# When the second gate pass starts, and how many of its steps stand in each v block

## The chip, the cores and the metric

The kernel runs on one core of a Trainium2 chip. The metric is the device time of one execution in microseconds. The core has a matrix engine (TensorE, PE in the profile), a vector engine (VectorE, DVE), a scalar engine (ScalarE, ACT), a general engine (GpSimd, POOL) and an engine that here issues transfers (SyncE, SP). Each has its own instruction stream, carried out in its written order; they wait for each other by semaphores. 16 DMA engines move data between HBM and on-chip memory.

## The reference

One decoder layer over 256 tokens of width 2048: attention in two head groups, a layer norm, a PEER block, a second norm, a gated per-layer embedding, and a third norm. All of it is in fp32. The change lies in the PEER block:

```
x   = LN1(alpha*x + concat(A, B) @ W_out)
q   = x @ peer_wq                      # 8 heads, two halves of 128
s1  = q[half 0] . keys[0] ; s2 = q[half 1] . keys[1]      # 128 keys each
top 16 of s1, top 16 of s2 -> 256 sums -> top 16          # per token and head
e   = ia*128 + ib                      # the expert's number, one of 16384
g   = softmax(the 16 sums)
h   = gelu(x . peer_u[e])              # one dot of 2048 per chosen expert
y   = sum over the 8*16 chosen of g*h*peer_v[e]
x   = LN2(alpha*x + y)
```

Every token thus needs 128 rows of `peer_u` and 128 rows of `peer_v`, 8 KB each.

## The kernel before, in words

**Two ways to do the experts.** Experts `e` are taken 128 at a time (a block, 1 MB of `peer_u` or `peer_v`). For most tokens the kernel computes whole blocks as matrix products: activations of all 128 experts of a block for all tokens (u part), multiplied by a gate matrix that is zero where a token did not choose the expert, then the product with the block's v rows (v part). A number of tokens (the natural or sparse ones) are done differently: their rows are gathered, one gather of 128 rows (1 MB, tile `gb`) at a time. 88 gathers of u rows each end in a dot on DVE (line 1012), 88 of v rows each in a step `y <- gb*ew + y` on DVE (line 1022). `gathers(n)`, called once a block with a table's number (`GU`, `GUL`, `GUE`, `GV`), spreads them over the blocks as background work; four `gb` tiles exist.

**Stages of the PEER block.** First the queries and their top 16, on DVE in `topk_work`, which also sends the sparse tokens' expert numbers to their slots (`head_slots`, transfers to `eig` issued by POOL). Then 56 direct u blocks (`u_block`), whose rows come in whole from SP's queue; their activations stand in the tiles A0 and A1. Then 48 listed u blocks: only experts that a token chose are in a list, and POOL's indirect DMA (`rows_of`, line 1409) fetches them by list into `uf` tiles; PE transposes them (1450) and multiplies them (1459), and the activations go to the tile `WL`. Then v: 39 blocks whose weights (`wc`) are gathered from the stored A0 and A1 (`s_w` in HBM), and 48 blocks whose weights are in `WL`; both by line 1505, sixteen matmuls a block, each against a 128-column piece of the block's rows (`vf` or `vx`). Five `vf` and `uf` tiles share slots; four `vx` tiles are used in the `wc` part.

**The gate passes.** `gate_work` makes the gate values for groups of three tokens. For each group DVE writes one-hots `eq` and `ohb` (line 717) and `lo` (1102), ACT writes `hi` (1100), PE multiplies them into a bank `ps_G` (1111, 1112), and DVE multiplies the activations by it (1120). The generator yields between these parts; a `run(work, n)` lets it go on by n steps. A full group takes two steps. Three or four groups are under way at a time. The first pass goes over A0 and A1 (56 groups) and, at the same time, finds each chosen expert's place in the list. Then A0 and A1 are stored to `s_w` (`stored = True`), the places are decoded, and the second pass (57 groups) goes over `WL`. In v, `half(d)` runs the second pass twice a block, after the eighth and the sixteenth matmul; the end of the pass must come before the first `WL` block.

**What sets the order.** DVE's and ACT's gate work and the y steps stand in the order in which the program text issues them (`keep`). PE's and POOL's instructions are placed by a planner at build time, and the placed order is fixed: an engine does not run ahead of an instruction that waits. In v two of the four banks used by `ps_G` hold sums of v, so that two are left for groups. POOL issues both the background gathers (line 1046) and all the blocks' fetches (1409) on one queue, one after another.

Of the kernel before, what the change touches and what calls it, by code (L numbers as in the profile page):

```python
# [19 lines left out]
P = 128  # L20
# [7 lines left out]
PH = 8  # L28
# [143 lines left out]
def build(tc, a, out):  # L172
# [7 lines left out]
    def pbank(pool, name, tag="bank", bufs=4):  # L180
        return pool.tile([P, 512], F32, name=name, tag=tag, bufs=bufs)
# [13 lines left out]
    at = pools.open("at", "left", bufs=2)  # L195
# [95 lines left out]
    def load(dst, src):  # L291
        tc.keep_in_program_order(nc.sync.dma_start(dst, src))
# [488 lines left out]
    def gates(t):  # L781

        g = gate[:, t]
        keep(nc.vector.tensor_tensor(g, CV[:, t], CV[:, t, :, 0:1].to_broadcast([P, PH, TOPK]),
                                     op=ALU.subtract))
        for _ in range(9):
            yield
        keep(nc.scalar.activation(g, g, AF.Exp))
        for _ in range(6):
            yield  # L790
        keep(nc.vector.tensor_reduce(gs[:, t], g, axis=AX.X, op=ALU.add))
        nc.vector.reciprocal(gs[:, t], gs[:, t])
        nc.vector.tensor_tensor(g, g, gs[:, t, :, None].to_broadcast([P, PH, TOPK]), op=ALU.mult)
        if t == 0:
            nc.vector.tensor_copy(eg[:NSPR, 1].bitcast(F32), g[:NSPR])
            for i in range(len(GROUPS)):
                slots(i, 1, by_slot(i, 1))
            gated.append(t)
        yield
# [3 lines left out]
    def slots(i, w, src):  # L803

        t0, n = GROUPS[i]
        nc.gpsimd.dma_start(eig[i][:, w],
                            src[t0:t0 + n].rearrange("t (r j) -> t r j", j=n))

    def by_slot(i, w):

        t0, n = GROUPS[i]

        buf, rows = (es, slice(t0, t0 + n)) if i < 2 else (es2, slice(GROUPS[1][0], NSPR))
        src = eg[rows, w].bitcast(F32)
        dst = buf[rows, w].bitcast(F32)
        nc.vector.tensor_copy(dst.rearrange("t (r h c) -> t h r c", h=PH, r=P // n),
                              src.rearrange("t h (r c) -> t h r c", r=P // n))
        return buf[:, w]

    def head_slots(h):  # L820

        c = slice(h * TOPK, (h + 1) * TOPK)
        nc.vector.scalar_tensor_tensor(eg[:NSPR, 0, h], iaN[:NSPR, 0, c], float(NKEY),
                                       ibN[:NSPR, 0, c], op0=ALU.mult, op1=ALU.add)
        t0, n = GROUPS[0]
        m = n // PH
        nc.gpsimd.dma_start(
            eig[0][:, 0, h * m:(h + 1) * m],
            eg[t0:t0 + n, 0, h].rearrange("t (r c) -> t r c", c=m))

    def topk_work():
        nc.vector.tensor_copy(io128, io128f)
        for h0, n in BATCH:
            for _ in topk_heads(0, h0, n):
                pass
            yield
            for h in range(h0, h0 + n):
                head_slots(h)
            yield
        for i in range(1, len(GROUPS)):  # L840
            slots(i, 0, by_slot(i, 0))

        second, first, flags = topk_heads(1, 0, PH), gates(0), first_flags()
        for step, _ in enumerate(second):
            if step > 2:
                next(first, None)
            if step > 5:
                next(flags, None)
            yield
        for _ in first:  # L850
            pass
        yield from index_T(1)
        yield from second_flags(gates(1), flags)

    def index_T(t):

        c = slice(t * P, (t + 1) * P)
        for src, dst, flat in ((iaN, iaT, iaF[:, c]), (ibN, ibT, None if t else ibF)):
            ps = pbank(pa, "ps_gT")
            keep(nc.tensor.transpose(ps[:, :P], src[:, t, :], ident))  # L860
            nc.scalar.copy(dst[:, c], ps[:, :P, None].to_broadcast([P, P, 2]))
            if flat is not None:
                nc.scalar.copy(flat, ps[:, :P])
            yield
# [28 lines left out]
    def first_flags():  # L893

        yield from index_T(0)
        cnt.append(pbank(pa, "ps_cnt")[:, :2 * P])
        keep(nc.tensor.matmul(cnt[0], ident, zero.to_broadcast([P, 2 * P]), start=True,
                              stop=False))
        for t0 in range(NSP, P, GB):
            n = min(GB, P - t0)  # L900
            oa, ob = (tkl.tile([P, GB, P], F16, name=nm, tag=nm) for nm in ("oa", "ob"))
            for j in range(n):
                act_one_hot(oa[:, j, :], tkl, iaF[:, t0 + j:t0 + j + 1])
                act_one_hot(ob[:, j, :], tkl, ibF[:, t0 + j:t0 + j + 1])
                if j or t0 % 5:
                    yield
            for j in range(n):
                count(t0 + j, ob[:, j, :], oa[:, j, :])
# [62 lines left out]
    def gathers(n):  # L971

        nonlocal due
        due += n
        while due >= 1:
            due -= 1
            run(sparse, 1)
# [222 lines left out]
    def all_gates(oh, A0, A1, WL):  # L1200

        places = Places(lkp, oh)
        yield from gate_work(oh, iaT, ibT, [(NSP, T, 0, SEG1, ((A0, NSP), (A1, NSP)))], places)
        a0 = 0
        for At in (A0, A1):
            for c in range(0, At.shape[1], 8):
                n = min(8, At.shape[1] - c)
                load(a["s_w"][1:, a0:a0 + n], At[:, c:c + n])
                a0 += n
                yield  # L1210
        nonlocal stored
        stored = True
        aT, bT = places.decode()
        yield
        nA, nB = CAPS[1]
        WA = WL[:, :nA * P].rearrange("p (b t) -> p b t", t=P)
        WB = WL[:, nA * P:].rearrange("p (b t) -> p b t", t=NDT)
        yield from gate_work(oh, aT, bT, [(NSP, P, nA, nB, ((WB, NSP),)),
                                          (P, T, 0, nA + nB, ((WA, P), (WB, NSP)))])
# [119 lines left out]
    def run(work, n):  # L1339

        for _ in range(n):
            if next(work, "end") == "end":
                return True
        return False


    def u_block(ia, dst):
        ps = pbank(pp, "ps_u")
        gemm_T32(su, a["peer_u"][ia], XF, ps, NSP, early[ia] if ia < EARLY else None)
        nc.scalar.activation(dst, ps[:, :NDT], AF.Gelu_apprx_tanh)  # L1350

    def W_of(ia):
        return A0[:, ia, :] if ia < SEG0 else A1[:, ia - SEG0, :]

    steps = 1
    work = topk_work()
# [26 lines left out]
    for ia in range(SEG1):  # L1383
        if ia == EARLY:
            pools.close("earlyp")
            a1p = pools.open("a1p", "right", bufs=1)
            A1 = a1p.tile([P, SEG1 - SEG0, NDT], F32, name="A1")
        u_block(ia, W_of(ia))
        run(work, steps + (steps == 1) * (ia % 2))
        gathers(0.9 if ia < EARLY else GU if steps == 1 else GUF if ia < SEG1 - 10 else GUT)  # L1390
    while not run(work, 1):
        pass
# [11 lines left out]
    def cols(i, b):  # L1404
        return (N0, P) if b < CAPS[i][0] else (0, NDT)
# [9 lines left out]
    def WL_of(b):  # L1415
        c0 = min(b, CAPS[1][0]) * P + max(b - CAPS[1][0], 0) * NDT
        return WL[:, c0:c0 + cols(1, b)[1]]
# [42 lines left out]
                             XF[:, d, NSP + c0:NSP + c0 + n], start=d == 0, stop=d == ND - 1)  # L1460

    stored = False
    work = all_gates(ohp, A0, A1, WL)
    rows = []
    turned = []

    def turn(k):
        b, c = divmod(k, 4)
        if b < NBLK[1]:
            if c == 0:  # L1470
                while len(rows) <= min(b + LEAD, NBLK[1] - 1):
                    rows.append(rows_of(slot("uf"), a["u_rows"], idxV[1], len(rows)))
            turned.append(rows_T(rows[b], c, pp, utp))
            if c == 3:
                rows[b] = None
# [3 lines left out]
    for b in range(NBLK[1]):  # L1479
        ps = pbank(pp, "ps_u")  # L1480
        c0, n = cols(1, b)
        for c in range(4):
            turn(4 * b + c + 2)
            rows_mm(ps, turned.pop(0), c, c0, n)
            if b >= 2 and (c or n > P) and not stored:
                run(work, 1)
        keep(nc.scalar.activation(WL_of(b), ps[:, :n], AF.Gelu_apprx_tanh))
        if b >= NBLK[1] - LEAD:
            fetch()
        gathers(GUL[n > P] if b < NBLK[1] - LEAD - 2 else GUE)  # L1490
# [46 lines left out]
    done = False  # L1537
    at = 0

    def half(d):  # L1540
        nonlocal done
        if not done:
            done = run(work, 1 + (d < 8 or at < 8))

    for b in range(NBLK[0]):
        if b == NBLK[0] - LEAD:
            more = nc.values_load(total[0:1, 0:1], min_val=0, max_val=NIA * NKEY)
        at = b
# [102 lines left out]
    with tc.If(more > 0, preferred_fallthrough_block=True, label="rest"):  # L1651
# [5 lines left out]
        for ia in range(NIA):  # L1657
            i = int(ia >= SEG1)
            vf, uf, _ = spare
# [397 lines left out]
```

## Time and profile before

| | |
|---|---|
| median of three runs | 1655.13 us (1651.96 to 1659.16) |
| profiled execution | 1654.64 us, span 1652.8 us |
| mean granted PE clock | 0.983 |
| PE, DVE, ACT, POOL busy | 97%, 64%, 44%, 35% of the span |
| DMA | 518.53 MB, mean 314 GB/s |
| direct u, listed u | about 560 to 816 us, 816 to 1132 us |
| v with `wc`, v with `WL` | 1136 to 1305 us, 1332 to about 1540 us |

Busy shares are averages over stages that have different limits. Times of stages are microseconds from the span's start, read from the timeline of PE. In a row of a timeline the first number is the start, the second the length; what stands in brackets at its end is the idle time before it and what ended it. `x` behind a row says how many instructions it groups. Waits are listed as total, count and longest.

### The profile page before, as it was taken

What the parts mean: (1) busy time and instruction counts of PE and PEld (TensorE: products, weight loads), DVE (VectorE), ACT (ScalarE), POOL (GpSimd) and SP (SyncE); (2) the same over time, 40 slices, a digit from 0 to 9 for tenths busy, and PEclk for the clock granted to TensorE, in tenths of its full rate; (3) what the DMA queues carried; (4) which work ended last, traced back from release to release, by engine and by line L of the source; (5) the groups of instructions that cost most, each with busy time, mean ns of one, the idle gap of its engine ahead of it and who ended that gap; (6) DMA issues with size and microseconds to landing.
All of it is one profiled execution on the core that took longest, in us unless ns stands there. A gap on an engine that the chain in (4) does not pass through costs nothing. (4 is left out here: it accounts for less than half of the span.)

```text
span 1652.8 us, 30585 instructions
## 1 busy us (share of the span) xinstructions
PE 1603.2 (97%) x11666; PEld 1486.8 (90%) x11666; DVE 1058.0 (64%) x2557; ACT 732.4 (44%) x1740; POOL 585.0 (35%) x542
## 2 busy tenths in 40 slices
PE   9999999999999999999989999999999679999998
PEld 7888888887888999999989999998999679999786
DVE  5555488855378899577678878842455762241776
ACT  5687458753101264857646666541032300000552
POOL 0133023201223423222464434447886455441000
PEclk9999999999999999999989999999999879999999
DMA  8554654485799799999999999999999899996661
GB/s 304 196 165 154 237 171 141 155 306 181 255 415 408 283 422 389 408 375 387 373 381 375 346 343 357 351 424 367 415 406 408 323 366 403 410 397 232 209 263 51
DMA packets 90614, 518.53 MB, mean 314 GB/s; under 512 B 12308, under 2 KB 15444, under 8 KB 38322
## 3 DMA queue, kind: packets, MB, share of 16 engines
q0 software_dynamic: 47984, 330.83, 50.9%
q1 hardware_dynamic: 40750, 182.55, 30.1%
q10 hardware_dynamic: 1728, 3.15, 0.5%
q8 instruction: 92, 1.51, 0.4%
q14 instruction: 60, 0.49, 0.1%
HBM read 508.47 MB, written 10.18 MB: 314 GB/s over the span
## 5 line engine op out<-in xcount | busy, mean ns | idle before, releaser
L133 DVE TENSOR_TENSOR wl<-wf,wh 128x1024 fp32r<-128x1024 f32 (+1 forms) x199 | 212.7, 1092 | 123.6 <-ACT wh L132 122.1
L132 ACT CAST wh<-wf 128x1024 fp32r<-128x1024 f32 (+1 forms) x199 | 172.1, 893 | 240.6 <-DMA wf<-ple_gate 128.7
L1022 DVE SCALAR_TENSOR_TENSOR y<-gb,ew,y 128x2048 f32<-128x2048 f32 x78 | 183.4, 2351 | 147.0 <-DMA gb<-v_rows,eig 146.6
L223 PE MATMUL ps_u<-XF,wf 128*128 128x168 f32 x1632 | 251.4, 310 | 1.5 <-DMA wf<-peer_u 1.4
L223 PEld LDWEIGHTS ps_u<-XF,wf 128*128 128x128 f32 x1632 | 234.5, 190 | 4.3 <-DMA wf<-peer_u 2.1
L1459 PE MATMUL ps_u<-XF,uT 128*128 128x128 f32 (+1 forms) x1536 | 222.5, 289 | 0.2 <-ACT uT L1453 0.2
L1012 DVE SCALAR_TENSOR_TENSOR gb<-gb,xq 128x2048 f32<-128x2048 f32 x88 | 200.7, 2285 | 21.3 <-DMA gb<-u_rows,eig 21.2
L1505 PE MATMUL ps_v<-WL,vf 128*128 128x128 f32 (+1 forms) x1536 | 197.1, 291 | 4.7 <-DVE WL L1120 4.5
L1459 PEld LDWEIGHTS ps_u<-XF,uT 128*128 128x128 f32 x1536 | 201.0, 193 | 0.5 <-ACT uT L1453 0.3
L1505 PEld LDWEIGHTS ps_v<-WL,vf 128*128 128x128 f32 x1536 | 195.3, 196 | 5.6 <-DVE WL L1120 4.7
L1046 POOL DMA_INDIRECT gb<-u_rows,eig x88 | 103.7, 1179 | 238.5 <-DVE gb L1012 56.5
L211 PE MATMUL ps_qk<-X,wh 128*128 128x512 f32 x512 | 185.2, 401 | 0.0
L1100 ACT ACTIVATE hi<-eq,ghf 128x56 f16<-128x56 f16 (+2 forms) x336 | 87.0, 325 | 166.0 <-DVE eq L717 162.1
L1453 ACT COPY uT<-ps_T 128x512 f32<-128x512 f32 x192 | 112.2, 587 | 109.2 <-PE ps_T L1450 109.0
L213 PE MATMUL ps_qk<-X,wl 128*128 128x256 f32 x512 | 145.7, 285 | 0.0
L1046 POOL DMA_INDIRECT gb<-v_rows,eig x88 | 121.5, 1381 | 66.2 <-DVE eq L717 24.0
L1409 POOL DMA_INDIRECT vf<-v_rows,idxV x73 | 90.3, 1237 | 114.3 <-PE ps_v L1505 84.0
L211 PEld LDWEIGHTS ps_qk<-X,wh 128*128 128x128 f32 x512 | 96.4, 188 | 22.0 <-issue 1.0
L1450 PE MATMUL ps_T<-ident,uf 128*128 128x128 f32 x768 | 115.1, 275 | 0.0
L223 PE MATMUL ps_q<-XF,wf 128*128 128x256 f32 x512 | 114.6, 382 | 0.0
L1505 PE MATMUL ps_v<-wc,vf 128*128 128x128 f32 (+1 forms) x800 | 106.4, 292 | 2.7 <-DMA vf<-v_rows,idxV 2.7
L223 PEld LDWEIGHTS ps_q<-XF,wf 128*128 128x128 f32 x512 | 96.4, 191 | 12.6 <-ACT eb L592 0.2
(366 smaller groups left out, 2855.2 us busy)
## 6 DMA issues: line engine op xcount, KB each, us to landing
wf<-peer_u SPq DMA_DIRECT2D x51, 1024.0 KB
wf<-w_qk SPq DMA_DIRECT2D x64, 512.0 KB
wf<-w_out SPq DMA_DIRECT2D x32, 512.0 KB
wf<-peer_wq SPq DMA_DIRECT2D x16, 1024.0 KB
wf<-ple_gate SPq DMA_DIRECT2D x16, 1024.0 KB
wf<-w_v SPq DMA_DIRECT2D x16, 512.0 KB
wf<-w_sv SPq DMA_DIRECT2D x15, 512.0 KB
early<-peer_u SPq DMA_DIRECT2D x5, 1024.0 KB
```

Of the source, the lines that this page charges most:

```text
L132: self.order(nc.scalar.copy(wh, src))
L133: self.order(nc.vector.tensor_tensor(wl, src, wh.bitcast(F32), op=ALU.subtract))
L211: nc.tensor.matmul(ps, wh[:, j * P:(j + 1) * P], xt[:, dt, :], start=dt == 0, stop=False)
L213: nc.tensor.matmul(ps[:, :T], wl[:, j * P:(j + 1) * P], xt[:, dt, :T], start=False, stop=dt == ND - 1)
L223: nc.tensor.matmul(ps[:, :T - t0], wf[:, dt * P:(dt + 1) * P], xt[:, dt, t0:], start=dt == 0, stop=dt == ND - 1)
L1012: keep(nc.vector.scalar_tensor_tensor(g, g, 1.0, xq[i], op0=ALU.mult, op1=ALU.mult, accum_out=eact[i][:, j:j + 1]))
L1022: keep(nc.vector.scalar_tensor_tensor(ys[i], g, ew[i][:, j:j + 1], ys[i], op0=ALU.mult, op1=ALU.add))
L1046: keep(nc.gpsimd.indirect_dma_start(out=g, out_offset=None, in_=a[kind], in_offset=bass.IndirectOffsetOnAxis(ap=eig[i][:, 0, j:j + 1], axi ...
L1450: nc.tensor.transpose(ps[:, j * P:(j + 1) * P], uf[:, (4 * c + j) * P:(4 * c + j + 1) * P], ident)
L1453: keep(nc.scalar.copy(uT, ps))
L1459: nc.tensor.matmul(ps[:, :n], uT[:, j * P:(j + 1) * P], XF[:, d, NSP + c0:NSP + c0 + n], start=d == 0, stop=d == ND - 1)
L1505: return nc.tensor.matmul(o, vf[:, d * P:(d + 1) * P], w, start=False, stop=last and (d % 3 == 2 or d == ND - 1))
```

## The change

Four edits, none of which changes what is computed.

1. In `topk_work` three more yields stand before the last batch's `head_slots`; three more steps are run in the first five direct u blocks.
2. The first gate pass starts at listed u block 4 where it started at block 2.
3. After the stores, one step of the second pass is run at the end of each listed u block, up to four (`begun`).
4. In v's first ten blocks `half` runs 3 + 2 steps a block, later 2 + 1; before, 2 + 2 in the first eight blocks, later 2 + 1.

```diff
@@ topk_work
             yield
+            if h0 + n == PH:
+                for _ in range(3):
+                    yield
             for h in range(h0, h0 + n):
                 head_slots(h)
             yield
@@ direct u blocks
-        run(work, steps + (steps == 1) * (ia % 2))
+        run(work, steps + (steps == 1) * (ia % 2 or ia < 5))
@@ listed u blocks
     stored = False
+    begun = 0
     work = all_gates(ohp, A0, A1, WL)
...
-            if b >= 2 and (c or n > P) and not stored:
+            if b >= 4 and (c or n > P) and not stored:
                 run(work, 1)
+        if stored and begun < 4:
+            begun += 1
+            run(work, 1)
@@ v, wc blocks
     def half(d):
         nonlocal done
         if not done:
-            done = run(work, 1 + (d < 8 or at < 8))
+            done = run(work, (3 if d < 8 else 2) if at < 10 else (2 if d < 8 else 1))
```

In the changed kernel all lines behind the first edit are higher by three to seven: 1409 is 1412, 1046 is 1049, 1111 is 1114, 1505 is 1512.

The instructions move most at three places. The first is POOL where listed u ends and v begins; `gb` is a background gather, `vf` and `vx` are rows of v blocks, `wc` their weights. Before:

```order
L1409 DMA vf<-v_rows,idxV_7967 128x2048
L1046 DMA gb<-v_rows,eig_4052 128x2048
L1409 DMA vf<-v_rows,idxV_7967 128x2048
L1046 DMA gb<-v_rows,eig_4052 128x2048
L1409 DMA vf<-v_rows,idxV_7967 128x2048
L1046 DMA gb<-v_rows,eig_4052 128x2048
L1409 DMA vf<-v_rows,idxV_7967 128x2048
L1409 DMA wc<-s_w,idxW 128x168 x5
```

and now:

```order
L1412 DMA vf<-v_rows,idxV_7967 128x2048
L1049 DMA gb<-v_rows,eig_4052 128x2048 x3
L1412 DMA vf<-v_rows,idxV_7967 128x2048
L1049 DMA gb<-v_rows,eig_4052 128x2048
L1412 DMA vf<-v_rows,idxV_7967 128x2048
L1049 DMA gb<-v_rows,eig_4052 128x2048 x4
L1412 DMA vf<-v_rows,idxV_7967 128x2048
L1412 DMA wc<-s_w,idxW 128x168 x5
```

Counted from the first gather of v rows, 36 gathers stood ahead of the first `wc` tile and 41 do now.

The second place is DVE behind the decoding of the places, which ends with `rowT`. Before, fifteen y steps stand ahead of the first group's one-hots, and all of the first four groups' follow each other:

```order
L1197 CAST rowT<-qj 128x336
L1022 SCALAR_TENSOR_TENSOR y_10082<-gb,ew_4054,y_10082 128x2048 x3
L1003 TENSOR_TENSOR ew_4062<-ew_4062,eig_4060 128x8
L1022 SCALAR_TENSOR_TENSOR y_10082<-gb,ew_4054,y_10082 128x2048 x12
L717 TENSOR_TENSOR eq<-io_4041,blkT 128x54
L717 TENSOR_TENSOR ohb<-io_4041,rowT 128x384
L1102 TENSOR_TENSOR lo<-eq,gl_4165 128x54
```

and now (the third group's, which follow these rows, stand behind two more y steps, and the fourth's behind nine more, at the place where the first's were, behind the 44th):

```order
L1200 CAST rowT<-qj 128x336
L717 TENSOR_TENSOR eq<-io_4041,blkT 128x54
L717 TENSOR_TENSOR ohb<-io_4041,rowT 128x384
L1105 TENSOR_TENSOR lo<-eq,gl_4165 128x54
L1025 SCALAR_TENSOR_TENSOR y_9971<-gb,ew_4054,y_9971 128x2048
L1006 TENSOR_TENSOR ew_4062<-ew_4062,eig_4060 128x8
L1025 SCALAR_TENSOR_TENSOR y_9971<-gb,ew_4054,y_9971 128x2048
L717 TENSOR_TENSOR eq<-io_4041,blkT 128x54
L717 TENSOR_TENSOR ohb<-io_4041,rowT 128x384
L1105 TENSOR_TENSOR lo<-eq,gl_4165 128x54
```

On PE, the first group's product moves into listed u and the second's to the start of v; the third's and fourth's stand behind 106 `wc` matmuls, where the first product stood behind 240.

The third place is PE at the end of the `wc` blocks, 16 matmuls each. Before, 70 gate matmuls stand between the last `wc` matmul and the first of the `WL` blocks; these are the last rows:

```order
L1111 LDWEIGHTS ohb
L1111 MATMUL ps_G<-hi,ohb 128x48
L1112 LDWEIGHTS ohb
L1112 MATMUL ps_G<-lo,ohb 128x48
L1505 MATMUL ps_v<-WL,vf 128x128 x112
```

and now:

```order
L1114 LDWEIGHTS ohb
L1114 MATMUL ps_G<-hi,ohb 128x48
L1115 LDWEIGHTS ohb
L1115 MATMUL ps_G<-lo,ohb 128x48
L1512 MATMUL ps_v<-wc,vf 128x168 x70
L1512 MATMUL ps_v<-WL,vf 128x128 x112
```

The gate product ends 70 matmuls of the `wc` part earlier than that part does.

## The prediction

> **What bounds the kernel now.** I read the page's busy times and its forty slices first.
>
> ```profile
> PE 1603.2 (97%) x11666; PEld 1486.8 (90%) x11666; DVE 1058.0 (64%) x2557; ACT 732.4 (44%) x1740; POOL 585.0 (35%) x542
> ...
> PE   9999999999999999999989999999999679999998
> ```
>
> TensorE (PE) is busy for 97% of the span, but two neighbouring slices fall to 6 and 7 tenths. Next came the windows of 25 us from the listed u to the end of v. Their columns are time, PE, PE weight load, VectorE (DVE), ScalarE, GpSimd (POOL), granted PE clock, mean DMA share, GB/s.
>
> ```profile
> 1075.00:1100.00 25.00, 25.00 (x192) 24.98 (x191) 9.44 (x9) 10.11 (x20) 12.77 (x9) 1.00 1.01 424
> 1150.00:1175.00 25.00, 22.30 (x185) 22.14 (x184) 9.41 (x4) 0.00 (x0) 20.40 (x16) 0.93 1.01 411
> 1275.00:1300.00 25.00, 25.00 (x223) 24.69 (x222) 19.18 (x63) 9.41 (x36) 8.82 (x6) 1.00 0.84 318
> 1300.00:1325.00 25.00, 9.42 (x109) 8.10 (x107) 19.93 (x53) 7.05 (x27) 10.21 (x8) 0.66 0.94 346
> 1325.00:1350.00 25.00, 17.97 (x139) 17.86 (x140) 20.02 (x20) 0.56 (x2) 16.58 (x11) 0.72 0.93 347
> 1350.00:1375.00 25.00, 25.00 (x227) 25.00 (x226) 5.32 (x3) 1.18 (x2) 12.70 (x11) 1.00 1.01 419
> ```
>
> PE has no idle time around 1075, 1275 and 1350; the hole is between 1300 and 1335, and DVE is at its busiest there (19.93 and 20.02 of 25). The DMA engines stand at 1.01 at the end of listed u, at the start of v and again behind the hole: whatever is moved forward in time there competes for a full queue. The waits of PE between 1100 and 1560 name the hole's cause (columns: total us, times, longest).
>
> ```profile
> PE ps_G L1111 <- DVE eq L717: 8.7, 4, 2.8
> PE ps_G L1111 <- DVE WL L1120: 7.2, 7, 2.7
> PE ps_v L1505 <- DVE WL L1120: 4.5, 1, 4.5
> PE ps_v L1505 <- DMA vf<-v_rows,idxV: 2.7, 1, 2.7
> ```
>
> The gate products wait for one-hots and scalings on DVE, each of which stands behind a 2.35 us y step in DVE's written order. PE has finished all its `wc` blocks by then; the first WL block needs the last scaling. The PE timeline gives the length of the tail (columns: start, us, instruction; a matmul in fp32 leaves two records).
>
> ```profile
> 1297.78 7.09 PE L1505 MATMUL ps_v<-wc,vf 128*128 128x168 f32 x48
> ...
> 1304.70 0.19 PE L1111 MATMUL ps_G<-hi,ohb 128*128 128x48 f16 x1
> ...
> 1304.98 0.18 PE L1112 MATMUL ps_G<-lo,ohb 128*128 128x48 f16 x1
> 1305.00 0.53 PE L1505 MATMUL ps_v<-wc,vf 128*128 128x168 f32 x2
> ...
> 1332.63 28.22 PE L1505 MATMUL ps_v<-WL,vf 128*128 128x128 f32 x224 [4.53 <-DVE WL L1120]
> 1361.12 7.31 PE L1505 MATMUL ps_v<-WL,vf 128*128 128x128 f32 x64
> ```
>
> **The tail goes (−28.5 us).** In the order of the change, the last gate product has 70 `wc` matmuls behind it where it had none. At 7.09 us for 48 records, that is 24 matmuls, a matmul is 0.295 us, so 70 of them take 20.7 us: time for the last scaling even behind one or two y steps. From the last `wc` matmul's end (1305.00 + 0.53) to 1332.63 are 27.1 us. The 70 gate matmuls in that stretch have to be done somewhere; twelve start between 1304.70 and 1304.98, 0.026 us each, so 1.8 us. The clock is still low behind the hole: 224 records took 28.22 us, while 64 took 7.31 at full clock, 0.112 each after the last one's length of some 0.17, so 25.0 us: 3.2 more. 27.1 − 1.8 + 3.2 = 28.5. It can be less if a scaling is late again: the last one stands behind the 57th to 59th of 88 y steps (62nd to 64th before), and the data of the 57th are asked for at least five blocks ahead. Bounds: 24 (one 4.5 us wait stays) to 28.5.
>
> **The start of v (+9 us).** The four early steps and the fifth step a block move the one-hots and, with them, gathers and y steps. In POOL's order five more gathers of 1 MB now stand ahead of the fetches of the `wc` tiles, as the rows shown with the change have it. What the start of v looked like on PE, POOL and DVE, and as GB/s in forty slices of 2 us from 1100 to 1180:
>
> ```profile
> 1132.08 4.69 PE L1511 MATMUL ps_v<-zero,ident 128*128 128x504 f32 x12
> 1136.61 14.45 PE L1505 MATMUL ps_v<-wc,vf 128*128 128x128 f32 x128
> 1153.76 5.44 PE L1505 MATMUL ps_v<-wc,vf 128*128 128x128 f32 x32 [2.70 <-DMA vf<-v_rows,idxV]
> ```
> ```profile
> 1116.46 2.18 POOL L1409 DMA_INDIRECT vf<-v_rows,idxV  x1 [2.84 <-PE ps_T L1450]
> ...
> 1122.78 0.99 POOL L1409 DMA_INDIRECT vf<-v_rows,idxV  x1 [2.88 <-PE ps_T L1450]
> 1124.08 1.01 POOL L1409 DMA_INDIRECT wc<-s_w,idxW  x1 [0.31 <-issue]
> ...
> 1142.98 1.00 POOL L1409 DMA_INDIRECT wc<-s_w,idxW  x1 [0.30 <-issue]
> 1144.28 0.96 POOL L1046 DMA_INDIRECT gb<-v_rows,eig  x1 [0.30 <-issue]
> 1145.55 1.00 POOL L1409 DMA_INDIRECT vf<-v_rows,idxV  x1 [0.30 <-issue]
> ```
> ```profile
> 1151.04 2.35 DVE L1022 SCALAR_TENSOR_TENSOR y<-gb,ew,y 128x2048 f32<-128x2048 f32 x1 [18.37 <-DMA gb<-v_rows,eig]
> 1156.27 4.81 DVE L1022 SCALAR_TENSOR_TENSOR y<-gb,ew,y 128x2048 f32<-128x2048 f32 x2 [2.88 <-DMA gb<-v_rows,eig]
> ...
> 1189.19 2.35 DVE L1022 SCALAR_TENSOR_TENSOR y<-gb,ew,y 128x2048 f32<-128x2048 f32 x1 [2.93 <-DMA gb<-v_rows,eig]
> 1191.46 0.18 DVE L717 TENSOR_TENSOR eq<-io,blkT 128x54 f16<-128x54 f16 x1
> ```
> ```profile
> GB/s 428 420 434 414 426 418 438 410 434 414 434 397 422 422 386 225 59 217 403 427 412 417 397 306 369 348 393 426 430 422 420 403 424 414 408 420 421 418 412 419
> ```
>
> A gather or a block of rows is 1.05 MB; at 419 to 424 GB/s that is 2.5 us of all the DMA engines. Five of them are 12.5 us. The queue had one hole before, the slices at 225, 59 and 217: about 3.6 us of 6 unused, because POOL was issuing small `wc` tiles. Filling it leaves 9 us by which the first `wc` tile, or the fifth block's rows (issued 1145.55, the cause of the 2.70 us wait), arrive later. PE meets this as a wait at one of v's first five blocks. Bounds: +3 (the 2.70 us wait, with the slow records behind it, turns out to hide part of the shift, and gathers land earlier in listed u) to +14.4 (the whole 12.5, and 1.9 of slow clock once more). That 1.9 is read here: 32 records took 5.44 us behind the wait, against 32 × 14.45/128 = 3.6.
>
> The next thing on PE is a written wait: twelve gate matmuls, groups 3 and 4, after 106 `wc` matmuls. Group 4's one-hots stand behind the 44th y step, and group 3's product needs a bank that is scaled behind them. Without a wait PE is there at 1136.61 + 106 × 2 × 14.45/128 = 1160.5. The 44th y step is now the third gather behind the burst of `wc` tiles; the third one before (the second of the two at 1156.27) ended at 1161.1. With 9 to 12.5 us for the shift it ends at 1170 to 1174, and PE, 9 us late, is at this place at 1169.5. So this wait lies behind the same delay, and I count 0 to 4 for it inside the bounds.
>
> **The start of the WL blocks (+6 us).** The hole at 1305 to 1335 was not empty for the DMA: POOL issued gathers through it. Counted in POOL's order, 57 gathers stood ahead of the first WL block's rows and 72 ahead of the 13th's; now it is 62 and 72. From the last `wc` matmul on there are 8 blocks and 7 gathers to move up to the 13th block (before: 8 and 2). At 2.5 us they take 37.5 us, and PE reaches the 13th block after 12 × 32 × 0.112 = 43 us. With an empty queue at the start nothing is late; with the fifth block and the four gathers that have buffers outstanding, 12.5 us, the 13th block is 7 late. Behind it 17 blocks and 8 gathers need 62.5 us against 61 of PE, so no debt is paid back. Bounds: 0 to +14 (all five more gathers and the 1.5). I take 6, near the queue with all buffers outstanding, because the windows of 1150 and 1350 show that queue full.
>
> **The first pass two blocks later (−2 us).** PE waited here for the first one-hots, which stand behind two dots on DVE; slow records followed.
>
> ```profile
> 844.89 2.29 DVE L1012 SCALAR_TENSOR_TENSOR gb<-gb,xq 128x2048 f32<-128x2048 f32 x1 [2.05 <-DMA gb<-u_rows,eig]
> ...
> 848.00 2.28 DVE L1012 SCALAR_TENSOR_TENSOR gb<-gb,xq 128x2048 f32<-128x2048 f32 x1
> ```
> ```profile
> 841.68 0.21 PE L1111 MATMUL ps_G<-hi,ohb 128*128 128x56 f16 x1 [7.41 <-DVE lo L1102]
> ...
> 842.61 2.07 PE L1459 MATMUL ps_u<-XF,uT 128*128 128x128 f32 x8 [0.17 <-ACT uT L1453]
> ...
> 847.95 1.06 PE L1459 MATMUL ps_u<-XF,uT 128*128 128x128 f32 x8
> ```
>
> Two more dots (eight, not six) now stand ahead of the one-hots. PE comes two blocks, about 12.6 us at 6.3 us a block in the listed part (POOL issues rows as PE frees them, at 1116.46 and 1122.78), after 841.68 − 7.41 = 834.3, at 847; the eighth dot ends at 850.3 and the one-hots 0.7 later. The wait is then 4 instead of 7.4. Because the two dots' gathers also stand later among the blocks' rows now, I take −2; bounds −9.4 (the wait and 2 us of slow clock go) and +4.
>
> **Slot transfers, and the added steps themselves (0).** SP's order is the same, and POOL's shows every slot transfer at its old place: the three extra yields are made up for by three extra steps in direct-u blocks 0, 2 and 4. The fifth step a block adds no instruction; it moves products between `wc` matmuls that take 0.026 us each, and DVE, which does the one-hots, was busy for 9.41 of 25 us at the start of v (the window at 1150). If that cover were gone, PE would wait for DVE at each group, as in the tail, up to 2.8 us each.
>
> **Sum.** −28.5 + 9 + 6 − 2 = −15.5. The profiled execution took 1654.64 us with a span of 1652.8; the median shown is 1655.13, 0.5 above it and inside the runs' own spread (1651.96 to 1659.16). 1654.64 − 15.5 = **1639 us**.
>
> [...]
>
> DVE's waits between 1100 and 1560 have one large row.
>
> ```profile
> DVE y L1022 <- DMA gb<-v_rows,eig: 135.3, 29, 18.4
> ```
>
> **Rivals.** *The full gain:* the queue takes the five gathers in its gaps; −28.5 + 3 + 0 − 2 = −27.5, 1627 us. For it: the queue's share is 0.84 in the window at 1275. Against: 1.01 in those at 1075, 1150 and 1350. *The queue takes it back:* both delays at their upper bounds, −28.5 + 14.4 + 14 − 2 = −2, 1652.5 us; for it the same three windows, against it the idle 3.6 us and the lead of four blocks that the rows have. *Slower, PE's written order:* the 44th y step does not come forward with its place in the queue. In the old trace it ended at 1191.5. If its gathers arrive as then and the burst comes 12.5 us later, it ends at 1204; PE stands from 1160.5, 43.5 us with 1.9 of slow clock behind, against 4.6 before (the wait of 2.70 with its own 1.9): +41, and −28.5 + 41 + 6 − 2 = +16.5, 1671 us. It decides against the kernel when that step ends later than about 1194 (a wait of 33.5 us). For it: DVE waited 135 us in all for these gathers. Against it: only two gathers and one block now stand between the burst and the 44th. *The change does nothing* would need the 70 `wc` matmuls not to cover the last scalings: the last of them behind a y step whose gather is late by over 20 us; 1655 us, and nothing but the upper end of the queue case speaks for it.
>
> **Chances.** Forecast (1629 to 1647) 0.57; full gain 0.08; queue takes it back or nothing left (1647 to 1663) 0.25; slower 0.10. A difference under 0.5%, 8.3 us, is what a measurement of this kernel cannot tell from none. Faster: 0.57 + 0.08 = 0.65; same 0.25; slower 0.10. The range takes most of the queue case in: 1628 to 1655.
>
> **What would show it.** Right: no gate product behind the last `wc` matmul and PE without idle time around 1305; a PE wait of 5 to 15 us at one of v's first seven blocks, named for `wc`, `vf` or the one-hots of the second pass; a few PE waits for `vf` in the first dozen WL blocks, 0 to 14 us together; the wait at the first pass between 0 and 8. Wrong: PE waits for scalings before the first WL block once more, a wait over 30 us at group 3, or a span that grows in the direct-u blocks, where I count nothing.

## The result, and the profile after

The changed kernel took 1646.05 us (median of ten runs, 1641.32 to 1653.21), the kernel before in the same ten rounds 1656.70. The ratio is 0.9941, with a 95% interval of 0.9927 to 0.9954: by it 9.8 us faster (the two medians differ by 10.7), where 15.5 were forecast. The profiled execution has a span of 1644.7 us against 1652.8, 8.1 less.

The waits of PE between 800 and 1560, after:

```profile
PE ps_v L1512 <- DMA vf<-v_rows,idxV: 11.7, 3, 8.2
PE ps_G L1114 <- DVE lo L1105: 8.7, 1, 8.7
PE ps_T L1453 <- ACT WL L1494: 5.8, 2, 4.6
```

No gate product of the second pass waits any more, and none stands before the first WL block. In their place are a longer wait for block rows (8.2 against 2.7 us) and a wait that the kernel before does not have: PE's transposes in listed u wait for ScalarE. The timeline of PE, at the places at which the prediction read it:

```profile
1113.56 1.12 PE L1453 MATMUL ps_T<-ident,uf 128*128 128x128 f32 x4 [4.63 <-ACT WL L1494]
1123.56 0.66 PE L1453 MATMUL ps_T<-ident,uf 128*128 128x128 f32 x4 [1.13 <-ACT WL L1494]
1138.61 4.69 PE L1518 MATMUL ps_v<-zero,ident 128*128 128x504 f32 x12
1143.29 14.54 PE L1512 MATMUL ps_v<-wc,vf 128*128 128x128 f32 x128
1166.01 5.52 PE L1512 MATMUL ps_v<-wc,vf 128*128 128x128 f32 x32 [8.18 <-DMA vf<-v_rows,idxV]
...
1299.41 20.20 PE L1512 MATMUL ps_v<-wc,vf 128*128 128x168 f32 x140
1319.45 18.03 PE L1512 MATMUL ps_v<-WL,vf 128*128 128x128 f32 x160
...
1360.00 5.47 PE L1512 MATMUL ps_v<-WL,vf 128*128 128x128 f32 x32 [3.37 <-DMA vf<-v_rows,idxV]
```

The `wc` matmuls run into the WL matmuls without a gap, 70 of them (140 records) without a gate matmul between. v itself starts late, at 1138.6 and not 1132.1, though this execution came to listed u 3.2 us early. Stage by stage, from the starts of the stages on PE:

| stage | before | after | difference |
|---|---|---|---|
| to the first listed u transpose | 815.93 | 812.72 | −3.2 |
| listed u, to v's zeroing matmuls | 316.15 | 325.89 | +9.7 |
| zeroing | 4.53 | 4.68 | +0.2 |
| v with `wc`, with the hole before | 196.02 | 176.16 | −19.9 |
| v with `WL`, to the sparse tokens' sums | 187.95 | 191.48 | +3.5 |
| sums to the end | 132.22 | 133.77 | +1.6 |
| span | 1652.8 | 1644.7 | −8.1 |

The loss in listed u is explained by ScalarE's timeline there, with VectorE's beside it:

```profile
1104.71 0.58 ACT L1456 COPY uT<-ps_T 128x512 f32<-128x512 f32 x1 [0.99 <-PE ps_T L1453]
1112.60 0.71 ACT L1103 ACTIVATE hi<-eq,ghf 128x18 f16<-128x18 f16 x3 [7.30 <-DVE eq L717]
1113.22 0.29 ACT L1494 ACTIVATE WL<-ps_u 128x168 f32<-128x168 f32 x1
1113.41 1.05 ACT L1456 COPY uT<-ps_T 128x512 f32<-128x512 f32 x2
```
```profile
1110.12 2.35 DVE L1025 SCALAR_TENSOR_TENSOR y<-gb,ew,y 128x2048 f32<-128x2048 f32 x1 [4.88 <-DMA gb<-v_rows,eig]
...
1112.39 0.18 DVE L717 TENSOR_TENSOR eq<-io,blkT 128x54 f16<-128x54 f16 x1
```

The early step's `hi` stands in ScalarE's order ahead of the block's activation and the `uT` copies. It waits 7.3 us for an `eq` that stands behind a y step, which waits for its gather. ScalarE does nothing else meanwhile. PE's next transposes start when the activation behind `hi` has ended (`WL` L1494 is the releaser in their row), so PE stops for 4.63 us. The next two sets of transposes and products behind the wait take 5.5 us at a granted clock of 0.57 (1113.56 to 1119.10); where PE had not stopped, two sets take 3.2 us at 1.00 (1102.41 to 1105.60).

Behind the start of v the queue is as full as before, and in the WL part it stays so up to 1470 (403 GB/s from 1440 to 1470, 303 in the 30 us after that):

```profile
1340.00:1365.00 25.00, 21.63 (x180) 21.44 (x179) 9.41 (x4) 1.18 (x2) 13.34 (x10) 0.93 1.01 420
1380.00:1405.00 25.00, 24.80 (x221) 24.58 (x220) 5.88 (x3) 0.00 (x0) 9.76 (x10) 1.00 1.01 421
```
```profile
vf<-v_rows,idxV POOLq DMA_INDIRECT x19, 13.4
```

The last row is from the DMA issues between 1300 and 1380: a block's rows take a median of 13.4 us from issue to landing. PE works off the four blocks that are ahead in an estimated 14.3 us (4 × 32 records of 0.112 us). Little room is left. GpSimd's own order is not what holds the rows back: in this window the time that it stands idle is mostly because PE has not yet freed the tile that the next rows go to.

```profile
POOL vf L1412 <- PE ps_v L1512: 28.4, 12, 6.4
```

### The profile page after: what moved, and what is told of

The parts are those of the page before. It is cut to its first block, busy times and chain, and to the rows that moved or that the text cites. A ratio compares the mean times of both kernels' runs of the same rounds, so it can differ in the third digit from the quotient of the medians.

```text
span 1644.7 us, 30592 instructions
## 1 busy us (share of the span) xinstructions
PE 1604.3 (98%) x11666; PEld 1488.5 (91%) x11666; DVE 1058.7 (64%) x2557; ACT 731.3 (44%) x1740; POOL 583.1 (35%) x542
## 5 line engine op out<-in xcount | busy, mean ns | idle before, releaser
L1049 POOL DMA_INDIRECT gb<-u_rows,eig x88 | 99.6, 1132 | 242.6 <-DVE gb L1015 59.7
L1412 POOL DMA_INDIRECT vf<-v_rows,idxV x73 | 93.9, 1286 | 120.6 <-PE ps_v L1512 88.2
L1049 POOL DMA_INDIRECT gb<-v_rows,eig x88 | 117.5, 1336 | 53.8 <-issue 20.7
L1512 PEld LDWEIGHTS ps_v<-wc,vf 128*128 128x128 f32 x800 | 102.6, 194 | 8.4 <-DMA vf<-v_rows,idxV 8.4
```

The source lines that it names most:

```text
L1049: keep(nc.gpsimd.indirect_dma_start(out=g, out_offset=None, in_=a[kind], in_offset=bass.IndirectOffsetOnAxis(ap=eig[i][:, 0, j:j + 1], axi ...
L1512: return nc.tensor.matmul(o, vf[:, d * P:(d + 1) * P], w, start=False, stop=last and (d % 3 == 2 or d == ND - 1))
```

## The experiments

Four theories were set against each other. A: each wait of TensorE counts by itself, and the loss in listed u is ScalarE's order. B and C: the early steps, or the fifth step a block, carry the gain alone. E: from the end of listed u on the DMA queue is full, so a stall that is removed comes back in part as waits for rows. Each theory's number stands in the text that was written before its run. The three groups of four ran on three chips; on the second and third the kernel before took 1677.4 and 1676.4 us, against 1658.7 on the first and 1656.7 in the runs on record, which are put with the first group for that reason. Ratios are compared inside a group. All stage lengths below are from one profiled execution each.

| kernel | ratio to before | listed u | `wc` part | `WL` part | gathers ahead of the first WL rows |
|---|---|---|---|---|---|
| kernel before, as on record | 1 | 316.2 | 196.0 | 188.0 | 57 |
| changed, as on record | 0.9941 (0.9927–0.9954) | 325.9 | 176.2 | 191.5 | 62 |
| fourth edit only | 0.9934 (0.9916–0.9951) | 318.4 | 181.7 | 192.4 | 57 |
| without the third edit | 0.9947 (0.9933–0.9961) | 316.7 | 180.7 | 194.1 | 57 |
| without the fourth edit | 0.9931 (0.9913–0.9950) | 324.4 | 177.2 | 187.9 | 62 |
| early steps at once | 0.9912 (0.9894–0.9929) | 315.8 | 173.5 | 195.3 | 60 |
| *second chip:* without the first edit | 0.9914 (0.9895–0.9934) | 325.8 | 190.2 | 189.9 | 62 |
| at once, first pass's one-hots early | 0.9948 (0.9929–0.9967) | 322.9 | 190.8 | 196.6 | 57 |
| at once, nine gathers left out | 0.9860 (0.9841–0.9880) | 316.1 | 192.1 | 184.9 | 60 |
| at once, gathers spread over listed u | 0.9862 (0.9843–0.9881) | 330.2 | 186.2 | 185.3 | 67 |
| *third chip:* changed kernel again | 0.9881 (0.9861–0.9902) | 326.1 | 188.7 | 192.4 | 62 |
| without the second edit | 0.9948 (0.9927–0.9969) | 327.1 | 192.7 | 193.4 | 62 |
| at once, WL gathers later | 0.9894 (0.9873–0.9915) | 316.8 | 191.3 | 189.5 | 60 |
| at once, spread, few before the first pass | 0.9797 (0.9775–0.9818) | 311.0 | 186.5 | 185.0 | 66 |

**The fourth edit alone.** The other three edits are undone.

```diff
-            if b >= 4 and (c or n > P) and not stored:
+            if b >= 2 and (c or n > P) and not stored:
...
-        if stored and begun < 4:
-            begun += 1
-            run(work, 1)
```

> Only the fourth edit is kept (five steps a block in v's first ten blocks); the other three are undone. Theory A (the listed part's loss comes from the early second-pass steps: ScalarE's hi waits for a one-hot and holds back the activation and copies behind it): no wait of TensorE for ScalarE in listed u, 36 gathers ahead of the first wc tile as before, so v starts as before. 28 gate matmuls stand behind the last wc matmul where the kernel before has 70, so about 28/70 of the 27.1 us hole stays, 11 us: 1656.7 - 16 = about 1640 us. Rival B (the early steps carry the gain, five steps a block alone only make the one-hots stand behind the same y steps): the hole stays at 20 us or more, about 1650 to 1655 us.

1646.58 us, a gain of 0.66% against the changed kernel's 0.59%: the intervals overlap, so one edit gives what all four give. It is 6.6 us short of theory A's 1640. PE waits for ScalarE nowhere in listed u, as theory A says. The `wc` part is 181.7 us, so 14 of the 20 us are won with 28 gate matmuls left behind the last `wc` matmul; but the WL part grew by 4.5 us against the kernel before, with three waits for rows of 1.13 us each, which theory A had not counted. Rival B is out.

**Without the early steps.** Only the `begun` lines are taken out.

> The changed kernel without the third edit (no step of the second pass in listed u). Theory A: the 5.8 us of waits of TensorE for ScalarE in listed u and some 2 us of slow clock behind them go, the 8.2 us wait for the fifth v block falls to about 3 to 5 because 37 and not 41 gathers stand ahead of the wc tiles; 28 gate matmuls are left behind the last wc matmul, 11 us. Sum against the changed kernel: -8 - 4 + 11 = about -1, so 1645 us. Rival B: the hole comes back with 20 us or more, about 1655 us.

1649.37 us, ratio 0.9947, 4 us above theory A's 1645. Listed u falls from 325.9 to 316.7 us: all of the loss there is the early steps' doing. Of the 9.2 us that it wins there it loses 7.1 in the `wc` part (180.7) and the WL part (194.1). The profiled execution was the fastest of the five (1643.03), so the stages show less of a loss than the times do.

**The old number of steps in v.**

```diff
-            done = run(work, (3 if d < 8 else 2) if at < 10 else (2 if d < 8 else 1))
+            done = run(work, 1 + (d < 8 or at < 8))
```

> The changed kernel with the old number of steps in v (2 + 2 in the first eight blocks, 2 + 1 later). Its order has only 4 gate matmuls behind the last wc matmul. Theory A (the early steps bring the second pass forward by enough, the fifth step only adds distance): waits in listed u and at v's start as in the changed kernel, up to 5 us for the last scaling: 1646 to 1651 us. Rival C (the fifth step carries the gain): about 1655 us.

1647.69 us, ratio 0.9931: no difference from the changed kernel. With the early steps the fifth step a block adds nothing that these times can tell, and with the fifth step the early steps add nothing. Rival C is out as well. Either edit removes most of the hole.

**The early steps at once.** The four steps run in one listed block, so the first three groups' one-hots follow the decoding with no y step between.

```diff
-        if stored and begun < 4:
-            begun += 1
-            run(work, 1)
+        if stored and not begun:
+            begun = 1
+            run(work, 4)
```

> The changed kernel with its four early steps run in one listed block, at once, so that the first three groups' one-hots follow the decoding directly on VectorE with no y step between them. Theory A: ScalarE's hi no longer waits for a y step's gather; the 5.8 us of waits of TensorE for ScalarE and about 2 us of slow clock go, and 39 instead of 41 gathers stand ahead of the wc tiles, up to 5 us less for the fifth v block: 1646 - 8 to 13 = about 1633 to 1638 us. Rival D (listed u is late because of the queue, not of ScalarE's order): the loss stays, about 1646 us, with the wait named for a DMA.

1644.54 us, ratio 0.9912. The waits for ScalarE are gone and listed u is 315.8 us, as long as in the kernel before: theory A's mechanism is shown, and rival D, which put the loss on the queue, is out. But 10 us won in listed u become some 5 in the time, with intervals that just meet, and the 1633 to 1638 us of theory A were not reached. The waits of PE between 800 and 1550 say where the rest went:

```profile
PE ps_v L1512 <- DMA vf<-v_rows,idxV: 11.7, 4, 4.2
PE ps_G L1114 <- DVE lo L1105: 7.6, 1, 7.6
PE ps_v L1512 <- DMA wc<-s_w,idxW: 3.7, 1, 3.7
```

PE now waits for the first `wc` tile, and 7.4 of the 11.7 us for `vf` lie in the WL part, which grew to 195.3 us. That is theory E's pattern, and the last column of the table has it in part: on this chip the changed kernels with 57 to 60 gathers ahead of the first WL rows need 192 to 195 us for the WL part, those with 62 need 188 to 191. The kernel before, with 57, needs only 188: it issued gathers while PE stood in the hole, so that 72 were ahead of the 13th WL block's rows, against 70 in those with 57 to 60. On the other two chips kernels with 62 range from 189.9 to 193.4, so the count alone does not settle it.

**Without the first edit.** The yields before `head_slots` and the steps that make up for them are undone.

> The changed kernel without its first edit (the three yields before the last slot transfers and the three steps that make up for them). No instruction of PE, SP, and only the place of single gathers differs, so theory A says 1646 us, as the changed kernel (ratio 0.994 within its interval). Rival F: the changed kernel reached listed u 3.2 us earlier than the kernel before because of this edit; then this one is 2 to 3 us slower, 1649 us, with the start of listed u at about 816 us.

Ratio 0.9914, on another chip. The changed kernel gave 0.9941 on the first chip and 0.9881 on the third, so this lies between; it did not run on this chip, so what the first edit is worth is not measured. Listed u starts at 817.5 us here; with the edit it starts between 812.7 and 819.1 in the profiles of the other kernels. Nothing speaks for rival F: the 3.2 us by which the profiled changed kernel was early lie inside this spread.

**The first pass's one-hots early.** On top of the steps at once:

```diff
+    run(work, 3)
     for k in range(2):
         turn(k)
```

> As e4 (the early second-pass steps at once) and, besides, the first three steps of the first pass before listed u's first block, so that their one-hots stand ahead of the dots on VectorE. The wait of 7.6 to 8.7 us at the first gate product goes, and some 2 us of slow clock with it; 16 gate matmuls stand behind the last wc matmul. Theory A alone (each wait of TensorE counts): e4's time less 9, about 1636 us. Theory E (from the end of listed u on the DMA queue is full, at about 420 GB/s, and the sums behind v start when the rows have come, whatever TensorE did before): less than half of it shows, 1640 to 1645 us, and the waits for vf grow.

Ratio 0.9948, worse than its group. The wait at the first gate product did not go: it came 20 us earlier and became longer, 10.5 us, because VectorE was still writing the lists then (to 824.7) and four dots of 2.28 us still stood ahead of the first one-hot (at 833.5). Listed u is 322.9 us. The experiment thus does not test theory E. Its WL part, with 57 gathers ahead, is the longest of all, 196.6 us.

**Nine gathers left out.** The 61st to 63rd and 66th to 71st gathers of v rows and their y steps are not done; the sparse tokens' sums lack these experts.

```diff
+                    if kind == "v_rows" and (i == 0 and 60 <= j < 63 or i == 1 and 1 <= j < 7):
+                        yield
+                        continue
```

> As e4, but 9 of the 88 gathers of v rows and their y steps are left out (the 61st to 63rd and the 66th to 71st, which fall at the end of the wc blocks and in the first WL blocks), so the sums of the sparse tokens lack these experts. Theory E: the WL part, 195 us in e4, 188 in the kernel before, falls back to 188, the waits for vf in it go, and the time falls by 6 to 9 us to about 1637 us. Theory A without a full queue: the waits for vf have another cause (the order of issues on GpSimd) and stay; no more than 2 us fall.

Ratio 0.9860. PE waits for rows nowhere behind 1330, and the WL part is 184.9 us. In the window in which the changed kernel's queue moved 420 GB/s, this one's has room:

```profile
1340.00:1365.00 25.00, 25.00 (x226) 25.00 (x226) 2.35 (x1) 0.59 (x1) 8.06 (x8) 1.00 0.93 344
```

So the waits of the WL part are the queue's, and the bytes that are asked for there cause them. How much they cost is less sure: the steps at once (195.3 us) ran on another chip; on the same chip the kernels with all gathers and 62 or 57 of them ahead have 189.9 and 196.6.

**Gathers spread over listed u.** The paces are changed on top of the steps at once.

```diff
-GUL, GUE = (1.10, 1.50), 2.20
+GUL, GUE = (1.25, 1.60), 1.6
```

> As e4 with another spread of gathers over listed u: 1.25 and not 1.10 a block in its first thirty blocks, 1.60 and not 1.50 in the next, and 1.60 and not 2.20 in its last six. 46 gathers stand ahead of the wc tiles where e4 has 39, but most of them are moved before the queue is full. Theory E: the queue has room in listed u (300 to 400 GB/s between 860 and 1070, 420 from 1075 on), so the waits for wc and vf at the start of v and in the WL part shrink by 8 to 12 us together: about 1634 us. Rival: the gathers cannot come earlier, because the four buffers and VectorE's order hold them; then TensorE waits for one-hots behind y steps in listed u or the wait at v's start grows by up to seven gathers, 17 us: 1645 to 1660 us.

Ratio 0.9862, against 0.9914 for the changed kernel without its first edit on the same chip; the intervals do not meet. The two differ in the steps at once as well as in the spread, so the spread's own share is not shown. No wait for `vf` or `wc` is left, and the WL part is 185.3 us with 67 gathers done ahead. The ratio is theory E's 1634 us almost to the figure, which is luck: a price that theory E had at nothing is in it. The rival had such a price, though at another place: more dots stand ahead of the first pass's one-hots.

```profile
PE ps_G L1114 <- DVE lo L1105: 16.4, 2, 13.3
```

**Without the second edit.** The first pass starts at listed block 2 again.

> The changed kernel without its second edit: the first pass starts at listed block 2 again. Theory A: the wait at the first gate product falls back from 8.7 to 7.4 us, the stores come 12 us earlier, which nothing waits for; so 1 us either way of the changed kernel on the same chip. Rival G: the later start is what pays for the early steps, and undoing it lets the waits of TensorE for ScalarE in listed u or for the one-hots grow: over 5 us slower than the changed kernel.

Ratio 0.9948 against 0.9881 for the changed kernel on the same chip: the second edit is worth 10 us there, which theory A had put at 1 and rival G at over 5. The wait at the first product is 8.5 and 8.2 us in the two profiles, and those for ScalarE in listed u are 7.1 and 7.0, so it is neither of these. In the `wc` part this kernel has 7.5 us of waits for a scaling that the changed kernel again does not have:

```profile
PE ps_G L1114 <- DVE WL L1123: 7.5, 4, 4.0
```

Why an earlier first pass makes the second pass's scalings late is not settled. The changed kernel's profiled execution was the longest of its six (1667.58 against a median of 1656.84), so the two profiles show less of the difference than the times do.

**Gathers later in the WL part.**

```diff
-GV = (0.42, 0.80), (0.42, 0.85)
+GV = (0.42, 0.80), (0.28, 1.08)
```

> As e4, but in the WL part 0.28 gathers a block in the first thirty blocks (0.42 before) and 1.08 in the last eighteen (0.85): some four gathers move from the WL part's first two thirds to its last third, all bytes stay. Theory E: in the first thirty blocks the queue (420 GB/s) and TensorE need about the same time, so four gathers less there, 10 us of the queue, take the 8 us of waits for vf away; in the last eighteen blocks a TensorE block takes 4.7 us and the queue has some room: the WL part falls from 195 to about 190, 5 us less than e4. Rival: the last gathers end too late and the sums behind v wait for them: no gain, with a wait at the sums.

Ratio 0.9894, the same as the changed kernel on this chip within the intervals. The steps at once with the old pace did not run on this chip, so the effect of the pace alone is open; the WL part, 189.5 us, and the 3.7 us left of waits for `vf` go the way theory E says.

**Spread, with few gathers before the first pass.** As the spread above, with 0.5 gathers a block in the first four listed blocks and 1.35 in the next.

```diff
-GUL, GUE = (1.10, 1.50), 2.20
+GUL, GUE = (1.35, 1.60), 1.6
...
-        gathers(GUL[n > P] if b < NBLK[1] - LEAD - 2 else GUE)
+        gathers(0.5 if b < 4 else GUL[n > P] if b < NBLK[1] - LEAD - 2 else GUE)
```

> As e11 (gathers spread over listed u), but 0.5 gathers a block in listed u's first four blocks and 1.35 in the next twenty-six (1.25 in both in e11). Fewer dots stand ahead of the first pass's first one-hots, so the wait at the first gate product, 13.3 us in e11, falls to under 5 us; the rest as in e11 (44 and not 46 gathers ahead of the wc tiles, 185 us in the WL part). 8 to 10 us less than e11: a ratio to the kernel before of about 0.981. Rival: VectorE's y steps among the gate steps of listed u hold the gate products back there once 1.35 gathers a block are asked for, and what is won at the first product is lost again: 0.986.

1642.59 us where the kernel before takes 1676.35: ratio 0.9797 (0.9775 to 0.9818), close to the 0.981 expected, and 14 us faster than the changed kernel on the same chip. Its waits of PE between 800 and 1550 are nearly empty:

```profile
PE ps_v L1512 <- issue: 7.4, 13, 1.1
PE ps_v L1512 <- DMA wc<-s_w,idxW: 2.7, 1, 2.7
PE ps_G L1114 <- DVE A L1123: 2.3, 1, 2.3
PE ps_G L1114 <- DVE WL L1123: 1.1, 1, 1.1
```

and the windows of listed u show a queue that moves more, first the changed kernel on this chip, then this kernel:

```profile
866.00:916.00 50.00, 50.00 (x566) 49.77 (x565) 39.00 (x151) 32.62 (x91) 20.03 (x18) 1.00 0.96 372
966.00:1016.00 50.00, 50.00 (x578) 49.73 (x577) 39.63 (x143) 32.34 (x91) 20.14 (x19) 1.00 0.90 340
```
```profile
866.00:916.00 50.00, 50.00 (x572) 49.75 (x572) 41.89 (x147) 32.52 (x90) 22.78 (x18) 1.00 1.00 408
966.00:1016.00 50.00, 50.00 (x559) 49.61 (x558) 43.27 (x145) 32.10 (x91) 27.45 (x20) 1.00 0.98 388
```

PE is as busy in both. Against the changed kernel's profile on this chip listed u is 15.2 us shorter and the WL part 7.4, while the start of v (zeroing and `wc` part) is 0.7 longer. So the larger part of the gain lies in listed u, where the waits for ScalarE (7.0 us) are gone and the one at the first product fell from 8.2 to 2.3. The WL part's share goes with gathers that the queue moved earlier, beside work that PE does anyway. The differences add up to more than 14 us because the changed kernel's profiled execution was its longest. This is the best version found.

## Why the prediction was right, and where it was wrong

The direction and the main term were right; the sum was 15.5 us, the measured gain 9.8, and one step was wrong. That the time still fell inside the range is in part luck: the loss that was not foreseen hid some of the start of v's, and the execution profiled came to listed u 3.2 us early.

- **The tail, −28.5.** Right. The `wc` part became 19.9 us shorter although its wait for rows grew by 5.5; with that and 1.8 us of gate matmuls between, the 27.1 us hole is gone. The first 160 records of the WL part take 18.03 us, full clock.
- **The early and the fifth steps themselves, 0.** This is the step that failed. I followed the early one-hots on VectorE, PE and POOL and left ScalarE out. Each early step also issues `hi` on ScalarE, in ScalarE's written order, ahead of the listed block's activation and copies. The two waits behind it, 5.8 us, with 2.3 us of slow clock after the first (5.5 against 3.2 us, as above) are most of the 9.7 us that listed u grew by, and the first pass has 1.3; running the steps at once took listed u back to 315.8 us.
- **The start of v, +9.** The mechanism was right, the term half hidden. The fifth block's rows came at 1166.0 and not 1153.8, 12.2 us later, against 9 forecast and 12.5 as a bound. PE had itself become 6.7 us late in listed u by then, so it met only 5.5 us more of wait. The two delays lie over each other, and that is why taking the first away, with the steps at once, won so little: the second came out. The wait for groups 3 and 4, counted at 0 to 4, did not appear in this execution.
- **The WL blocks, +6.** Right: 3.6 us of waits for `vf`, and 5.47 us for the 32 records behind the longer one, which take 3.6 at full clock. Together 5.5. The stage shows 3.5 more: the 3.2 us of slow clock, counted in the tail, went out of it, which leaves 2.3; the other 1.2 us are not placed.
- **The first pass, −2.** Measured +1.3: the wait is 8.7 against 7.4 us, outside the 0 to 8 of the prediction's signs. The dots ended at 850.0, as forecast (850.3), but PE was there at 841.9 and not at 847. Two blocks were counted at 6.3 us each, read at the end of listed u; at its start the blocks' transposes follow each other at 5.44 us (824.13, 829.57, 835.01), and this execution was 3.2 us early. On the third chip the edit is worth 10 us by another way, which no term had.

```profile
847.70 2.29 DVE L1015 SCALAR_TENSOR_TENSOR gb<-gb,xq 128x2048 f32<-128x2048 f32 x1 [2.67 <-DMA gb<-u_rows,eig]
```
```profile
850.66 0.21 PE L1114 MATMUL ps_G<-hi,ohb 128*128 128x56 f16 x1 [8.73 <-DVE lo L1105]
```

- **The slot transfers, 0.** Nothing in the runs speaks against it, but the one run without them has no counterpart on its chip.
- **The clock.** The 2.70 us wait before was followed by 32 records in 5.44 us at a granted clock of 0.69, the 3.37 us wait at 1360 by 5.47 at 0.69 and the 8.18 us wait by 5.52 at 0.68, where 32 records take 3.6 at 1.00; in the kernel without the first edit a wait of 2.41 us was followed by 5.47. But 2.93 us in the steps at once and 2.86 us with the WL gathers later were followed by 3.84 at a clock of 1.00. So the length of such a wait alone does not decide, and the 1.9 us that the prediction put behind a wait held for some waits and not for others.
- **The rivals.** None of the four came. The queue did take gain back, as in the second, but in part: the fifth block's rows came as late as the bound had it, but PE met only 5.5 us more of wait, and the WL blocks cost 5.5 of at most 14. The 44th y step, the last ahead of the fourth group's `eq`, ended at 1174.1, at the end of the 1170 to 1174 that the prediction worked out, so the slower case did not arise. (Its limit of 1194 leaves out the +6 of the WL blocks; with it the same terms give 1188.) The rows:

```profile
1171.79 2.35 DVE L1025 SCALAR_TENSOR_TENSOR y<-gb,ew,y 128x2048 f32<-128x2048 f32 x1 [0.93 <-DMA gb<-v_rows,eig]
1174.06 0.18 DVE L717 TENSOR_TENSOR eq<-io,blkT 128x54 f16<-128x54 f16 x1
```

## What to carry to other kernels

A step that is moved to an earlier place has to be followed on every engine on which it issues an instruction, the lightly loaded one too: here ScalarE, busy for 44% of the span, stood 7.3 us at a blocked `hi`, and PE, which needed an instruction behind it in ScalarE's order, stood 4.6 us. Where the DMA queue is full behind a stall, as in the WL part here (1.01, 420 GB/s), removing the stall can give back less than its length: of the 10 us that the steps at once won in listed u some 5 showed in the time. The best kernel here has transfers moved ahead as well, into a stage where the queue had room (listed u, 372 and 340 GB/s in the changed kernel, 408 and 388 in the best one). And two edits that each remove most of the same hole were worth one here (0.9934 with the one, 0.9931 with the other, 0.9941 with both), which only undoing them one by one showed.

## What the runs showed of the hardware that was not expected

The same kernel differs between the three groups' chips by more than the change is worth: the kernel before by about 20 us (1677.4 and 1676.4 against 1656.7). On the second and third chip PE has small gaps in v's first blocks that the profile puts down to nothing but issue, 6.9 to 11.9 us in all in every kernel that was profiled there, and none on the first chip. The row of the changed kernel on the third chip, then how it looks on PE's timeline:

```profile
PE ps_v L1512 <- issue: 11.9, 17, 2.2
```
```profile
1164.48 0.37 PE L1512 MATMUL ps_v<-wc,vf 128*128 128x128 f32 x1 [0.94 <-issue]
1165.20 0.78 PE L1512 MATMUL ps_v<-wc,vf 128*128 128x128 f32 x2 [0.34 <-issue]
```

Its `wc` part is 188.7 us there and 176.2 in the profile on record. The gaps come while the queue works off the burst of `wc` tiles: in the kernel without the first edit they lie between 1158 and 1192, 17 `wc` tiles are issued between 1140 and 1200, and the DMA share is 1.00 to 1.01 from 1155 to 1195. What they are is open; no run was aimed at them. The change is worth 0.59% in the runs on record and 1.19% on the third chip, where the same 0.6% had been expected, with intervals that do not meet, so a ratio of this kernel holds for the group of runs in which it was taken. Each group ran on one chip at one time, so it is not shown that the chip is the cause.
